# Two-term operands in every fourth value block, values loaded by pairs, the second norm's transposes under the output projection, and finer decode steps, in a hybrid encoder layer with expert retrieval

## Chip, cores and metric

The kernel runs on one core of a Trainium2 chip. The metric is the device time of one execution in microseconds. Its engines are named as in the profile: PE multiplies matrices (PEld loads its weights), DVE and ACT do elementwise work, POOL small elementwise work and the indirect loads, SP issues most transfers. Sixteen transfer engines serve all queues. A change of about 0.2% is the smallest that a measurement of this kernel can tell.

## What is computed

One encoder layer for two sequences of 256 tokens (a prompt, s = 0, and a sample, s = 1), width 1024, all in f32:

```
h = concat(meta, x)                                  # 16 meta tokens ahead, dropped at the end
z = rmsnorm(h) @ w_in                                # conv gates and q, k, v
y = concat(norm(gated_conv3(z)), norm(attention(z))) # 8 heads, 2 kv heads
h = h + y @ w_out
xn = rmsnorm(h)                                      # the second norm
s = einsum(xn @ wq, subkeys)                         # 8 heads x 2 halves x 128 keys
top 16 of each half, top 16 of the 256 sums          # picks 16 of 16384 experts per head
gates = softmax(picked scores)
a = gelu(u[idx] . xn) * gates                        # 128 experts per token
h = h + sum(a * v[idx])
```

u and v are tables of 16384 x 1024 f32, 67 MB each. The scores decide which experts are picked, so they need close to f32 accuracy.

## The kernel before

The two sequences take different ways through the expert tables.

**Sequence 0, gathered.** For each token tile of 128 tokens (t = 0, 1) and each of its 128 picks per token, one indirect load (L157) brings 128 rows of 8 KB (a row of u and of v side by side) into a ring of GBUF = 4 buffers. DVE takes the dot with x (`g_dot`, tile grow), ACT the gelu and the gate (`g_weight`, tile dots), DVE adds the value row times the weight to hg (`g_val`). That makes 256 gathers. They are spread over the whole of the work for sequence 1: `bg(us)` stands behind each piece of PE work, adds us times a share to a credit, and calls `gather()` for each GU = 2.65 of it. The first call fills the ring; each later one does one dot, the value of the gather before it, and one issue. Each issue also waits for the last matmul recorded in `pe_mark`. After the last dot and value of t = 0 the accumulator is stored, and x and hg are loaded anew for t = 1, by POOL (L166 to L168, L190).

**Sequence 1, dense.** All 16384 experts are computed: block j of 128 has 16 PE instructions pSj = u_j x (the u loop, L867), gelu on ACT, a product with the gate matrix A(j); then in the v loop (L893) acc += A(j) v_j, four f32 matmuls of 128x512, which are eight PE instructions of two passes each. The gate matrix is scattered from the picks by `gates_dense` (L802): decode of the picks for both tiles, then 64 steps that build one-hot operands on DVE and multiply them on PE (pgm, L848).

**Order.** The instruction order within each engine is what the code emits, with a planner that may move ready work ahead; a gather's dot is pinned behind DVE's last instruction emitted before it. Long work for DVE is written as generators with a price at each `yield`: `run_tasks` goes on with the task while a second credit is not negative. The stages are: front(0) with operands split in two f32r terms (three products, one pass each, in place of the f32 pair of two passes), projections and top-k of sequence 0; front(1) with gathers at share SF = 0.5 and top-k and decode of tile 1 as a task at SB0 = 0.35; the projections of sequence 1 (share SR = 0.6) with step1 for the top-k of each head; the u loop with share SS = 0.64 (0.7 once the dense steps are done) and the dense steps at SBS = 0.42; the v loop, in which the remaining gathers (`left`) are dealt out evenly over 126 blocks.

**Second norm.** At the end of `front`, four slices of w_out (L676) are added to h; in the last slice `hold` keeps gathers back, the sum of squares gives the scale, DVE forms x = h * scale * g (L696), and `norm_T` (L698) turns it: 16 PE transposes (pt, L416) with ACT copies to xr, and for s = 0 the low term xrl on DVE. Then the projections `pqq` with wq start.

**Buffers.** Weights, u blocks and most v blocks share four buffers of 4 KB per partition (`wtile`); every third v block is in one of two buffers vp, so six in all. The S accumulators of the u loop have four PSUM buffers.

```
875          n = tau[0]
876          if n:
877              act.activation(p[:, :n], p[:, :n], AF.Gelu)
878              dve.tensor_tensor(A(j)[:, :n], p[:, :n], A(j)[:, :n], op=ALU.mult)
904          want = left * (j + 1) // (P - 2)
905          while done < want:
906              gather()
```

Of the kernel before, what the change touches and what calls it, by code (L numbers as in the profile page):

```python
# [18 lines left out]
P = 128  # L19
# [20 lines left out]
SS = 0.64  # L40
SMAX = 0.7
SBS = 0.42


@with_exitstack
def encoder_layer(ctx: ExitStack, tc: tile.TileContext, xp, xs_, meta, vec, w_in, w_out, wq,
# [25 lines left out]
    def sb(name, bufs, side="left"):  # L72
        return tc.tile_pool(name=name, bufs=bufs, side=side, reuse_waits="tile")
# [5 lines left out]
    drm = ctx.enter_context(tc.tile_pool(name="drm", bufs=1, space=DRAM))  # L79
    wp = ctx.enter_context(sb("wp", 4))  # L80
    selp = ctx.enter_context(sb("sel", 1, "right"))
    gc = ctx.enter_context(sb("gc", 1, "right"))
    ga = ctx.enter_context(sb("ga", GBUF, "right"))

    ident = cst.tile([P, P], F32, name="ident")
# [126 lines left out]
    GU = 2.65  # L212
    hold = [False]

# [7 lines left out]
    def bg(us):  # L222
        if tasks:
            credit["b"] += us * share["b"]
            run_tasks(1)
        credit["a"] += us * (share["a"] if tasks else min(share["a"] + share["b"], SMAX))
        while credit["a"] >= GU and not hold[0]:
            credit["a"] -= GU
            gather()


    def retrieval(pools, sv, si, cv, cp, gs, scores, t0, lkbuf, dc):

# [29 lines left out]

        def gates(t):
            ge_ = gate_all[:, t0 + t].rearrange("p (h k) -> p h k", k=KTOP)
            dve.tensor_tensor(ge_, cv[:, t], cv[:, t, :, 0:1].to_broadcast([P, PH, KTOP]), op=ALU.subtract)
            act.activation(gate_all[:, t0 + t], gate_all[:, t0 + t], AF.Exp)
            dve.tensor_reduce(gs[:, t], ge_, axis=AX.X, op=ALU.add)
            dve.reciprocal(gs[:, t], gs[:, t])
            dve.tensor_tensor(ge_, ge_, gs[:, t, :, None].to_broadcast([P, PH, KTOP]), op=ALU.mult)  # L270

        def lookup(mask, tab2, out):
            w = lkbuf(0)
            if tab2 is None:
# [12 lines left out]

        def decode(t):
            s16 = t2.tile([P, 16, KTOP], F16, tag="s16", name="s16", bufs=1)
            dve.tensor_copy(s16, si[:, t])  # L290
            c16 = t2.tile([P, PH, KTOP], F16, tag="c16", name="c16", bufs=1)
            dve.tensor_copy(c16, cp[:, t])
            s4 = s16.rearrange("p (h q) k -> p h q k", q=2)
            di = t2.tile([P, PH, KTOP, 2], F16, tag="di", name="di", bufs=1)
            dj = t2.tile([P, PH, KTOP, 2], F16, tag="dj", name="dj", bufs=1)
            for r in range(2):
                dve.tensor_copy(di[:, :, 0, r], s4[:, :, 0, 0])
                dve.tensor_tensor(di[:, :, 1:, r], s4[:, :, 0, 1:], s4[:, :, 0, :-1], op=ALU.subtract)
# [4 lines left out]
            lookup(mk, di, idx_i[:, t].rearrange("p (h k) -> p h k", k=KTOP))  # L303
            yield 6.0
            b16 = t2.tile([P, PH, KTOP], F16, tag="b16", name="b16", bufs=1)
            lookup(mk, None, b16)
            dve.tensor_tensor(b16, c16, b16, op=ALU.subtract)
            yield 4.0
# [3 lines left out]
            lookup(mk2, dj, idx_j[:, t].rearrange("p (h k) -> p h k", k=KTOP))  # L312
# [23 lines left out]

    def projections(xr, sk, scores, qp, step=None, split=False):

        late = []

        def key_scores(hp, qs):
            pn = pst.tile([P, 2, P], F32, tag="tr", name="pn")
            for t in range(2):
                pe.matmul(pn[:, t, :], qs[:, t * P:(t + 1) * P], sk[:, hp, :], start=True, stop=True)
            act.activation(scores[:, hp], pn, AF.Copy)
            if step is not None and hp % 2:
                step(hp // 2)

        for hd in range(PH):
            w = weights(wq, hd, split)  # L350
            for pp in range(2):
# [69 lines left out]

    def front(s, h):

# [249 lines left out]
        if sp:  # L673
            xrl = [r0t.tile([P, 4, 256], F32R, tag=f"lk{i}", name=f"xrl{i}", bufs=1) for i in range(2)]
        xs2 = []
        for sl in range(4):  # L676
            hold[0] = sl == 3
            w = weights(w_out, sl, sp)
            for t in range(2):
# [5 lines left out]
                act.activation(sq, hsl, AF.Square, accum_out=ss2[:, t, sl:sl + 1])  # L685
                bg(3.5)
                if sl == 3:
                    sst = tmp.tile([P, 2], F32, tag="sst", name="sst")
                    dve.tensor_reduce(sst[:, 0:1], ss2[:, t], axis=AX.X, op=ALU.add)
                    rsqrt(sst[:, 1:2], sst[:, 0:1], 1, 1.0 / D)  # L690
                    if s == 0 and t == 0:
                        x = gc.tile([P, D], F32, tag="xg", name="xg0")
                        gctx["x"] = x
                    else:
                        x = tmp.tile([P, D], F32, tag="xs", name="xs")
                    dve.scalar_tensor_tensor(x, h[:, t, :], sst[:, 1:2], gf, op0=ALU.mult, op1=ALU.mult)  # L696
                    xs2.append(x)
        for t in range(2):  # L698
            tok = slice(t * P, (t + 1) * P)
            norm_T(lambda c: xr[:, c, tok], xs2[t], (lambda c: xrl[c.start // 4][:, :, tok]) if sp else None)  # L700
        hold[0] = False
        if s == 0:
# [11 lines left out]

    xr0 = front(0, hs_)

# [16 lines left out]

    heads0, fin0, _ = retrieval(r0t, *picks(r0p, "p0"), sc0, 0, lk0, dc0)

# [16 lines left out]
    share.update(a=SF, b=SB0)  # L752
    xr1 = front(1, hs1)

# [33 lines left out]
    def step1(hd):  # L788
        for _ in heads1(hd, [0, 1]):
            pass  # L790
        topk_left[0] -= 1

    share.update(a=SR, b=0.0)
    projections(xr1, sk1, sc1, q1, step1)
    pfs.close()
# [94 lines left out]
    hd_ = gc.tile([P, 2, D], F32, tag="xr", name="hd")  # L890
    left = len(queue) + len(pend)
    done = 0
    for j in range(P):  # L893
        vb = vp.tile([P, D], F32, tag="v", name="v") if j % 3 == 2 else wtile("v")
        nc.sync.dma_start(vb, vn3[:, j])
        if j == P // 2:
            for t in range(2):
                act.dma_start(hd_[:, t, :], hdram[1 + t])
        for t in range(2):
            for q in range(2):  # L900
                i = pe.matmul(acc[t][q], A(j)[:, t * P:(t + 1) * P], vb[:, q * 512:(q + 1) * 512],  # L901
                              start=j == 0, stop=j == P - 1, skip_group_check=True)
# [80 lines left out]
```

## Time and profile before

| what | value |
|---|---|
| median of 3 runs | 1390.26 us (1388.64 to 1391.82) |
| profiled execution, its own time | 1388.95 us |
| its span, first to last instruction | 1387.0 us |
| PE busy, share of the span | 1309.7 us, 94% |
| DVE busy | 1032.9 us, 74% |
| ACT, POOL busy | 433.9 us, 424.7 us |
| moved by transfers | 460.19 MB, mean 332 GB/s |
| granted PE clock, mean | 0.984 |

The shares are means over stages with different limits, so the page's totals don't tell what one stage waits for. The stages by time: front(0) and its projections to about 200 us, front(1) to about 340, the projections of sequence 1 to about 414, the u loop to 924, the v loop to 1383. Times in the rows of a timeline are us from the span's start; in brackets stands how long the engine was idle before, and on whose end.

### The profile page before, as it was taken

The page shows a single profiled execution, that of the slowest core. Times are in us where ns is not written, and L with a number is a line of the kernel's source. Part 1 is how long each engine was busy: PE and PEld are TensorE (multiplying, and loading weights), DVE is VectorE, ACT ScalarE, POOL GpSimd, SP SyncE. Part 2 cuts the span into 40 slices and gives each one's busy share as a digit, 9 for nine tenths or more (in the row PEclk, how much of TensorE's full clock was granted, in tenths as well). Part 3 has the DMA queues.
Part 4 walks back from the last instruction along what each step waited for, and adds up shares of the span by engine and source line. Part 5 has one row for each costly group of instructions (what it writes and reads, how often), then busy time and mean ns, then how long its engine had stood idle before and what let it go on. Part 6 is the DMA issues. An engine that isn't in the chain of part 4 may idle for free. (4 is left out here: it accounts for less than half of the span.)

```text
span 1387.0 us, 17651 instructions
## 1 busy us (share of the span) xinstructions
PE 1309.7 (94%) x5868; PEld 931.2 (67%) x5868; DVE 1032.9 (74%) x2349; ACT 433.9 (31%) x1456; POOL 424.7 (31%) x481
## 2 busy tenths in 40 slices
PE   5998998998989997799999999989999999999998
PEld 5888996676868886688888888854443334444433
DVE  5656899785899785888888899476666666666665
ACT  4554532732222211455555544121111111111111
POOL 2111124341344322212222222233454543334431
PEclk9999999999999999899999999999999999999999
DMA  6434536578888998799999999999999999999997
GB/s 213 128 120 136 181 113 237 211 274 313 311 309 296 409 396 305 305 365 358 363 361 359 371 357 388 366 417 417 416 417 416 417 417 416 416 417 415 417 417 311
DMA packets 90234, 460.19 MB, mean 332 GB/s; under 512 B 10512, under 2 KB 11024, under 8 KB 57120
## 3 DMA queue, kind: packets, MB, share of 16 engines
q0 software_dynamic: 37296, 270.02, 49.0%
q1 hardware_dynamic: 50832, 182.33, 35.5%
q10 hardware_dynamic: 2016, 6.72, 1.4%
q8 instruction: 46, 0.75, 0.2%
q14 instruction: 44, 0.36, 0.1%
HBM read 454.81 MB, written 4.19 MB: 331 GB/s over the span
## 5 line engine op out<-in xcount | busy, mean ns | idle before, releaser
L157 POOL DMA_INDIRECT grow<-in_uv,eidx x256 | 345.6, 1350 | 692.6 <-DMA grow<-in_uv,eidx 142.4
L130 PE MATMUL pSj<-xr,u 128*128 128x256 f32 x2048 | 466.2, 385 | 10.6 <-ACT Al L63 6.6
L130 PEld LDWEIGHTS pSj<-xr,u 128*128 128x128 f32 x2048 | 387.7, 192 | 65.2 <-ACT Al L63 8.7
L63 DVE SCALAR_TENSOR_TENSOR grow<-grow,xg 128x1024 f32<-128x1024 f32 x256 | 312.4, 1221 | 149.5 <-DMA grow<-in_uv,eidx 145.6
L63 DVE SCALAR_TENSOR_TENSOR hg<-grow,dots,hg 128x1024 f32<-128x1024 f32 x256 | 328.0, 1281 | 80.0 <-ACT dots L63 77.6
L901 PE MATMUL acc<-v,Al 128*128 128x512 f32 x752 | 335.4, 599 | 3.3
L901 PEld LDWEIGHTS acc<-v,Al 128*128 128x128 f32 x752 | 138.9, 190 | 199.2 <-issue 154.3
L63 ACT ACTIVATE dots<-dots 128x1 f32<-128x1 f32 x256 | 51.5, 202 | 564.8 <-DVE grow L63 564.6
L901 PE MATMUL acc<-v,Ah 128*128 128x512 f32 x272 | 119.1, 596 | 1.4 <-DMA v<-in_v_n 1.0
L901 PEld LDWEIGHTS acc<-v,Ah 128*128 128x128 f32 x272 | 50.8, 190 | 69.8 <-issue 58.8
L63 ACT ACTIVATE gl<-oj,glo 128x128 f16<-128x128 f16 x256 | 89.1, 393 | 12.0 <-DVE oj L63 5.8
L63 ACT ACTIVATE dots<-dots,gate_all 128x1 f32<-128x1 f32 x256 | 75.0, 294 | 7.4 <-ACT dots L63 0.4
L63 ACT ACTIVATE pSj<-pSj 128x256 f32<-128x256 f32 (+40 forms) x93 | 26.1, 281 | 126.2 <-PE pSj L130 126.2
L63 DVE TENSOR_TENSOR wlo<-w,whi 128x1024 fp32r<-128x1024 f32 x42 | 51.0, 1217 | 19.1 <-ACT whi L63 13.1
L130 PE MATMUL pqq<-xr,w 128*128 128x256 f32 x256 | 59.8, 388 | 0.0
L130 PEld LDWEIGHTS pqq<-xr,w 128*128 128x128 f32 x256 | 48.8, 196 | 6.7 <-ACT xr L63 0.2
L63 ACT ACTIVATE whi<-w 128x1024 fp32r<-128x1024 f32 x42 | 44.0, 1056 | 23.2 <-PE pqq L130 12.2
L848 PE MATMUL pgm<-gh,oi 128*128 128x128 f16 x256 | 35.9, 220 | 13.7 <-DVE gh L63 13.6
L130 PE MATMUL pc<-xT,w 128*128 128x258 f32 (+1 forms) x192 | 47.4, 390 | 1.1 <-DVE rb L63 0.6
L130 PEld LDWEIGHTS pc<-xT,w 128*128 128x128 f32 x192 | 34.8, 191 | 8.7 <-issue 2.5
L130 PE MATMUL pqq<-xr,whi 128*128 128x256 f32 x128 | 37.6, 297 | 0.0
L130 PE MATMUL pqq<-xrl,whi 128*128 128x256 f32 x128 | 36.7, 287 | 0.0
(261 smaller groups left out, 1536.1 us busy)
## 6 DMA issues: line engine op xcount, KB each, us to landing
u<-in_u_t SPq DMA_DIRECT2D x128, 512.0 KB
v<-in_v_n SPq DMA_DIRECT2D x128, 512.0 KB
w<-in_w_in SPq DMA_DIRECT2D x36, 512.0 KB
w<-in_wq SPq DMA_DIRECT2D x32, 512.0 KB
w<-in_w_out SPq DMA_DIRECT2D x16, 512.0 KB
grow<-in_uv,eidx POOLq DMA_INDIRECT x256
hdram<-h ACTq DMA_DIRECT2D x3, 512.0 KB
h<-in_xp SPq DMA_DIRECT2D x2, 512.0 KB
```

Source lines behind the costliest of these rows:

```text
L63: i = f(*a, **k)
L130: i = pe.matmul(out, st_(c, a), mv(c, b), start=(n == 0), stop=(n == NC * len(terms) - 1))
L157: i = pool.indirect_dma_start(out=r, out_offset=None, in_=uv, in_offset=bass.IndirectOffsetOnAxis(ap=eidx[:, t, k:k + 1], axis=0))
L848: pe.matmul(pg[:, r, :], oi[:, k, :], gh[:, k, :], start=True, stop=False)
L901: i = pe.matmul(acc[t][q], A(j)[:, t * P:(t + 1) * P], vb[:, q * 512:(q + 1) * 512], start=j == 0, stop=j == P - 1, skip_group_check=True)
```

## The change

1. In the v loop every fourth block (j % 4 == 3) has A(j) and v_j in two f32r terms each, high and low, and three products of one pass each: 12 matmuls in place of eight instructions. ACT makes the high terms, DVE the low ones, one block ahead of PE.
2. Two v blocks are loaded by one transfer (8 KB per partition), into three buffers of that size; the weight buffers are closed before the v loop.
3. At the end of `front` the transposes take h itself, slice by slice, under the next slice's matmuls (`turn`); the gain goes in as a scale of the copy on ACT, and the row scale rn later: for s = 0 in the softmax of the gates, for s = 1 by `rescale`, which scales the first two key scores on copying and then multiplies xr in place by the scale, broadcast over partitions by a matmul. `hold` is gone; x is only formed for s = 0.
4. `decode` yields after smaller pieces.
5. In the projections of sequence 1 the steps of step1 give the gathers' credit (`more`), and `bg` gives none from the first of them on.
6. hd is loaded at the end of the v loop.

```diff
+SPL = 4
...
+    def more(us):
+        credit["a"] += us
+        while credit["a"] >= GU:
             credit["a"] -= GU
             gather()
...
-            act.activation(gate_all[:, t0 + t], gate_all[:, t0 + t], AF.Exp)
+            act.activation(gate_all[:, t0 + t], gate_all[:, t0 + t], AF.Exp, scale=1.0 if rn is None else rn[:, t:t + 1])
...
+            yield 2.4
             n = 8
             while n > 1:
                 dve.tensor_tensor(w[:, :, 0:n, :], w[:, :, 0:n, :], w[:, :, n:2 * n, :], op=ALU.add)
                 n //= 2
             dve.tensor_tensor(out, w[:, :, 0, :], w[:, :, 1, :], op=ALU.add)
+            yield 1.6
...
+            yield 1.8
             mk = lkbuf(1)
...
-            yield 6.0
+            yield from lookup(mk, di, idx_i[:, t].rearrange("p (h k) -> p h k", k=KTOP))
...
-            yield 5.0
+            yield 0.3
...
+            if hp < 2 and rn is not None:
+                for t in range(2):
+                    act.activation(scores[:, hp, t], pn[:, t], AF.Copy, scale=rn[:, t:t + 1])
+            else:
+                act.activation(scores[:, hp], pn, AF.Copy)
...
+                if hd == 0 and rescale is not None:
+                    rn = rescale(xr, pp)
                 bg(3.9)
...
+        def turn(sl):
+
+            pt = pst.tile([P, 2, 256], F32, tag="tr", name="pt")
+            for c in range(2):
+                for t in range(2):
+                    o = (2 * sl + c) * P
+                    pe.transpose(pt[:, c, t * P:(t + 1) * P], h[:, t, o:o + P], ident)
+            for c in range(2):
+                k = 2 * sl + c
+                act.activation(xr[:, k], pt[:, c], AF.Copy, scale=vecs[:, 8 + k:9 + k])
+                if sp:
+                    dve.scalar_tensor_tensor(xrl[k // 4][:, k % 4], pt[:, c], vecs[:, 8 + k:9 + k], xr[:, k].bitcast(F32),
+                                             op0=ALU.mult, op1=ALU.subtract)
+
         for sl in range(4):
-            hold[0] = sl == 3
...
-                bg(3.5)
...
+                if t == 0 and sl:
+                    turn(sl - 1)
+                if sl < 3 or t == 0:
+                    bg(3.5)
+        turn(3)
         for t in range(2):
...
+            dve.tensor_reduce(rn[:, t:t + 1], ss2[:, t], axis=AX.X, op=ALU.add)
+        rsqrt(rn, rn, 2, 1.0 / D)
+        bg(3.5)
...
     def step1(hd):
-        for _ in heads1(hd, [0, 1]):
-            pass
+        share["a"] = 0.0
+        for us in heads1(hd, [0, 1]):
+            more(us * SR)
...
+    def rescale(xr, pp):
+
+        if pp == 0:
+            on = q1.tile([P, P], F32, name="on", bufs=1)
+            pool.memset(on, 1.0)
+            dg = q1.tile([P, 2, P], F32, name="dg", bufs=1)
+            for t in range(2):
+                act.activation(dg[:, t], ident, AF.Copy, scale=rn1[:, t:t + 1])
+            pb = pss.tile([P, 512], F32, tag="sc", name="pb")[:, :256]
+            pe.matmul(pb, on, dg.rearrange("p t n -> p (t n)"), start=True, stop=True)
+            rows.append(pb)
+        else:
+            for c in range(NC):
+                dve.tensor_tensor(xr(c), rows[0], xr(c), op=ALU.mult)
+        return rn1
...
-    vp = ctx.enter_context(sb("vp", 2, "right"))
+    wpx.close()
+    vp = ctx.enter_context(sb("vp", 3, "right"))
+    ap_ = ctx.enter_context(sb("ap", 1, "right"))
...
+    def values(j):
+
+        if j % 2 == 0:
+            vpair[0] = vp.tile([P, 2, D], F32, tag="v", name="v") if j else v0
+            nc.sync.dma_start(vpair[0], vn3[:, j:j + 2])
+        vb = vpair[0][:, j % 2]
+        if j % SPL != SPL - 1:
+            return ((A(j), vb),)
+        vh, vl = vhl[:, 0], vhl[:, 1]
+        ah = ap_.tile([P, 256], F32R, tag="ah", name="ah")
+        al = ap_.tile([P, 256], F32R, tag="al", name="al")
+        act.activation(ah, A(j), AF.Copy)
+        act.activation(vh, vb, AF.Copy)
+        dve.tensor_tensor(al, A(j), ah.bitcast(F32), op=ALU.subtract)
+        dve.tensor_tensor(vl, vb, vh.bitcast(F32), op=ALU.subtract)
+        return ((ah, vh), (al, vh), (ah, vl))
+
+    nxt = values(0)
     for j in range(P):
-        vb = vp.tile([P, D], F32, tag="v", name="v") if j % 3 == 2 else wtile("v")
-        nc.sync.dma_start(vb, vn3[:, j])
...
+        terms = nxt
+        nxt = values(j + 1) if j + 1 < P else None
+        for n, (a, v) in enumerate(terms):
             for t in range(2):
+                for q in range(2):
+                    i = pe.matmul(acc[t][q], a[:, t * P:(t + 1) * P], v[:, q * 512:(q + 1) * 512],
+                                  start=j == 0 and n == 0, stop=j == P - 1 and n == len(terms) - 1, skip_group_check=True)
...
+    hd_ = vp.tile([P, 2, D], F32, tag="v", name="hd")
+    nc.sync.dma_start(hd_, hdram[1:3].rearrange("t p d -> p t d"))
```

More of the change, by code (lines that the diff above doesn't have):

```diff
@@ L79, in encoder_layer @@
     drm = ctx.enter_context(tc.tile_pool(name="drm", bufs=1, space=DRAM))
-    wp = ctx.enter_context(sb("wp", 4))
     selp = ctx.enter_context(sb("sel", 1, "right"))
@@ L83, in encoder_layer @@
     ga = ctx.enter_context(sb("ga", GBUF, "right"))
+    wpx = ExitStack()
+    wp = wpx.enter_context(sb("wp", 4, "right"))
     ident = cst.tile([P, P], F32, name="ident")
@@ L212, in encoder_layer @@
     GU = 2.65
-    hold = [False]
     def run_tasks(limit=None):
@@ L226, in bg, with retrieval @@
         credit["a"] += us * (share["a"] if tasks else min(share["a"] + share["b"], SMAX))
-        while credit["a"] >= GU and not hold[0]:
+        more(0.0)
+    def more(us):
+        credit["a"] += us
+        while credit["a"] >= GU:
             credit["a"] -= GU
             gather()
-    def retrieval(pools, sv, si, cv, cp, gs, scores, t0, lkbuf, dc):
+    def retrieval(pools, sv, si, cv, cp, gs, scores, t0, lkbuf, dc, rn=None):
         t2 = pools
@@ L302, in decode @@
                               dc[:, 0:1].to_broadcast([P, PH, 16, 16]), op=ALU.is_ge)
-            lookup(mk, di, idx_i[:, t].rearrange("p (h k) -> p h k", k=KTOP))
-            yield 6.0
+            yield from lookup(mk, di, idx_i[:, t].rearrange("p (h k) -> p h k", k=KTOP))
             b16 = t2.tile([P, PH, KTOP], F16, tag="b16", name="b16", bufs=1)
-            lookup(mk, None, b16)
+            yield from lookup(mk, None, b16)
             dve.tensor_tensor(b16, c16, b16, op=ALU.subtract)
-            yield 4.0
             mk2 = lkbuf(1)
@@ L311, in decode @@
                               dc[:, 2:3].to_broadcast([P, PH, 16, 16]), op=ALU.is_equal)
-            lookup(mk2, dj, idx_j[:, t].rearrange("p (h k) -> p h k", k=KTOP))
+            yield from lookup(mk2, dj, idx_j[:, t].rearrange("p (h k) -> p h k", k=KTOP))
             if t0 == 0:
                 dve.scalar_tensor_tensor(eidx[:, t], idx_i[:, t], 128.0, idx_j[:, t], op0=ALU.mult, op1=ALU.add)
-            yield 5.0
+            yield 0.3
         def head_steps(hd, tiles):
@@ L335, in retrieval, with projections @@
         return head_steps, fin_steps, all_steps
-    def projections(xr, sk, scores, qp, step=None, split=False):
+    def projections(xr, sk, scores, qp, step=None, split=False, rescale=None):
+        rn = None
         late = []
@@ L344, in key_scores @@
                 pe.matmul(pn[:, t, :], qs[:, t * P:(t + 1) * P], sk[:, hp, :], start=True, stop=True)
-            act.activation(scores[:, hp], pn, AF.Copy)
+            if hp < 2 and rn is not None:
[3 more added lines that the diff above has]
+                act.activation(scores[:, hp], pn, AF.Copy)
             if step is not None and hp % 2:
@@ L420, in norm_T, with front @@
                 dve.tensor_tensor(dst_lo(cs), pt, dst(cs).bitcast(F32), op=ALU.subtract)
-    def front(s, h):
+    def front(s, h, rn):
         sp = s == 0
@@ L674, in front @@
             xrl = [r0t.tile([P, 4, 256], F32R, tag=f"lk{i}", name=f"xrl{i}", bufs=1) for i in range(2)]
-        xs2 = []
+        def turn(sl):
[10 more added lines that the diff above has]
+                                             op0=ALU.mult, op1=ALU.subtract)
         for sl in range(4):
-            hold[0] = sl == 3
             w = weights(w_out, sl, sp)
@@ L685, in front @@
                 act.activation(sq, hsl, AF.Square, accum_out=ss2[:, t, sl:sl + 1])
-                bg(3.5)
[L687 to L697, printed above, removed]
-        for t in range(2):
-            tok = slice(t * P, (t + 1) * P)
-            norm_T(lambda c: xr[:, c, tok], xs2[t], (lambda c: xrl[c.start // 4][:, :, tok]) if sp else None)
-        hold[0] = False
+                if t == 0 and sl:
[3 more added lines that the diff above has]
+        turn(3)
+        for t in range(2):
+            dve.tensor_reduce(rn[:, t:t + 1], ss2[:, t], axis=AX.X, op=ALU.add)
+        rsqrt(rn, rn, 2, 1.0 / D)
+        bg(3.5)
+        xs2 = []
+        if s == 0:
+            for t in range(2):
+                x = gc.tile([P, D], F32, tag="xg", name="xg0") if t == 0 else tmp.tile([P, D], F32, tag="xs", name="xs")
+                dve.scalar_tensor_tensor(x, h[:, t, :], rn[:, t:t + 1], gf, op0=ALU.mult, op1=ALU.mult)
+                xs2.append(x)
+            gctx["x"] = xs2[0]
         if s == 0:
@@ L713, in front @@
         return lambda c, k=0: xr[:, c]
-    xr0 = front(0, hs_)
+    rn0 = r0p.tile([P, 2], F32, name="rn0")
+    xr0 = front(0, hs_, rn0)
     hs1 = one.tile([P, 2, D], F32, tag="h", name="h1")
@@ L732, in lk0 @@
         return r0t.tile([P, PH, 16, 16], F16, tag=f"lk{i}", name=f"lk{i}", bufs=1)
-    heads0, fin0, _ = retrieval(r0t, *picks(r0p, "p0"), sc0, 0, lk0, dc0)
+    heads0, fin0, _ = retrieval(r0t, *picks(r0p, "p0"), sc0, 0, lk0, dc0, rn0)
     def step0(hd):
@@ L752, in encoder_layer @@
     share.update(a=SF, b=SB0)
-    xr1 = front(1, hs1)
+    rn1 = selp.tile([P, 2], F32, name="rn1")
+    xr1 = front(1, hs1, rn1)
     pf.close()
@@ L788, in step1 @@
     def step1(hd):
-        for _ in heads1(hd, [0, 1]):
-            pass
+        share["a"] = 0.0
+        for us in heads1(hd, [0, 1]):
+            more(us * SR)
         topk_left[0] -= 1
+    rows = []
+    def rescale(xr, pp):
[3 more added lines that the diff above has]
+            dg = q1.tile([P, 2, P], F32, name="dg", bufs=1)
+            for t in range(2):
+                act.activation(dg[:, t], ident, AF.Copy, scale=rn1[:, t:t + 1])
[6 more added lines that the diff above has]
+        return rn1
     share.update(a=SR, b=0.0)
-    projections(xr1, sk1, sc1, q1, step1)
+    projections(xr1, sk1, sc1, q1, step1, rescale=rescale)
     pfs.close()
@@ L889, in encoder_layer @@
     vn3 = v_n.rearrange("(i j) d -> i j d", j=P)
-    hd_ = gc.tile([P, 2, D], F32, tag="xr", name="hd")
+    vhl = gc.tile([P, 2, D], F32R, tag="xr", name="vhl")
     left = len(queue) + len(pend)
     done = 0
+    v0 = [vp.tile([P, 2, D], F32, tag="v", name="v") for _ in range(3)][-1]
+    vpair = [v0]
+    def values(j):
[14 more added lines that the diff above has]
+    nxt = values(0)
     for j in range(P):
-        vb = vp.tile([P, D], F32, tag="v", name="v") if j % 3 == 2 else wtile("v")
-        nc.sync.dma_start(vb, vn3[:, j])
-        if j == P // 2:
+        terms = nxt
+        nxt = values(j + 1) if j + 1 < P else None
+        for n, (a, v) in enumerate(terms):
             for t in range(2):
[L898 to L902, printed above, removed]
+                for q in range(2):
+                    i = pe.matmul(acc[t][q], a[:, t * P:(t + 1) * P], v[:, q * 512:(q + 1) * 512],
+                                  start=j == 0 and n == 0, stop=j == P - 1 and n == len(terms) - 1, skip_group_check=True)
         pe_mark[0] = i
```

## The prediction

> **What bounds the kernel now.** I read the busy times by stretches first (stretch, length, busy us with instruction count of PE, PEld, DVE, ACT, POOL, then granted clock, DMA share, GB/s), then the chain that ended last.
>
> ```profile
> 160.00:180.00 20.00, 20.00 (x173) 20.00 (x172) 19.79 (x100) 10.28 (x20) 3.58 (x21) 1.00 0.54 159
> 340.00:440.00 100.00, 92.35 (x437) 80.43 (x438) 89.77 (x435) 23.05 (x76) 38.24 (x73) 0.95 0.82 301
> 600.00:860.00 260.00, 259.93 (x1513) 226.74 (x1512) 228.86 (x466) 135.77 (x562) 58.08 (x58) 1.00 0.96 363
> 923.96:1372.00 448.04, 443.42 (x1001) 185.07 (x999) 291.81 (x350) 57.49 (x232) 187.16 (x115) 1.00 1.02 417
> ```
>
> The u loop (600 to 860) is PE's: no idle, 363 GB/s. The v loop begins at 923.96, and there both are full: PE nearly so, the transfers at a share of 1.02 and 417 GB/s. Which of them sets its end? The chain (start, length, what):
>
> ```profile
> 1046.38 3.71 PE acc L901 x8
> 1050.09 0.02 issue
> 1050.11 18.90 DMA v<-in_v_n
> ...
> 1270.18 58.65 PE acc L901 x136
> ...
> 1383.22 0.69 DVE hd L63
> ```
>
> Unhindered, an instruction takes 58.65/136 = 0.431 us, a block of eight 3.45, 128 blocks 441.6. The loop takes 1383.2 - 924.0 = 459.2, so PE's own floor is 17.6 us below it. What stands between is a landing of v: 18.90 and then 3.71 of one block, 22.7 us for the six buffers, 3.78 us a block. Now the bytes (counts from the loop's tiles):
>
> ```profile
> L157 POOL DMA_INDIRECT grow<-in_uv,eidx x115: 936/1910/1959, 925.1 to 1365.7; - x115
> ...
> L895 SPq DMA_DIRECT2D v<-in_v_n x123: 327/328/328, 924.2 to 1362.1; - x123
> ```
>
> 123 loads of 0.524 MB and 115 gathers of 1.049 MB (128 rows of 8 KB) are 185 MB; 417 GB/s for 448.0 us moves 187 (hd is most of the rest). **The transfers bound the v loop**, and PE comes 4% behind them. Time is gained there by moving bytes ahead of it, hardly by a faster PE.
>
> **The change, part by part**, against the profiled execution's 1388.95 us (its span of 1387.0 and 1.95 around it); the median of the runs, 1390.26, is 1.3 higher.
>
> *Fewer gathers in the v loop.* A gather is called for each 2.65 us of credit. Before: front 1 gives 107.2 x 0.5 = 53.6, the projections 16 x 3.9 x 0.6 = 37.4, the u loop 114 x 2.24 + 14 x 2.45 = 289.7 (0.64 x 3.5 a block while dense steps last, then 0.7 x 3.5). 380.7/2.65 is 143 calls, of which the first only issues: 142 done, 114 left. After: the steps of step1 give 8 x (2.9 + 2.9 + 3.5) x 0.6 = 44.6, and bg only its first two calls, 4.7; decode's yields sum to 14.1 for 15, so the dense steps end at block 112, not 114, and the u loop gives 290.1. 393.0/2.65 is 148 calls, 109 left. **Five gathers, 5.24 MB at 417 GB/s: -12.6 us.** Without hold, two calls only come somewhat earlier.
>
> *Operands in two terms.* 32 blocks get 12 matmuls for 8 instructions. A single pass of 512 columns is not in the trace. The first row above has 20/173 = 0.116 us for 256 columns in one pass; so 0.116 and 0.431 bound it, and I take 0.216, half the f32 instruction (nearest, with the same 512 columns, and about twice 0.116). 12 x 0.216 = 2.59 for 3.45: PE's floor falls by 27.5 to 414 us. While the transfers need about 435 I cost it at nothing. What it adds on other engines, by rows of the same shapes:
>
> ```profile
> L63 DVE TENSOR_TENSOR wlo<-w,whi 128x1024 fp32r<-128x1024 f32 x42 | 51.0, 1217 | 19.1 <-ACT whi L63 13.1 <-PE pc L130 5.6
> ...
> L63 ACT ACTIVATE whi<-w 128x1024 fp32r<-128x1024 f32 x42 | 44.0, 1056 | 23.2 <-PE pqq L130 12.2 <-PE pc L130 3.2 <-PE po L130 3.0
> ...
> L63 DVE TENSOR_TENSOR h<-po,h 128x256 f32<-128x256 f32 x16 | 6.5, 419 | 6.5 <-PE po L130 6.5
> ```
>
> ACT 1.06 and some 0.4 for ah, DVE 1.22 + 0.42 = 1.64. DVE's cycle of a gather:
>
> ```profile
> 1043.56 1.22 DVE L63 SCALAR_TENSOR_TENSOR grow<-grow,xg 128x1024 f32<-128x1024 f32 x1 [0.66 <-DMA grow<-in_uv,eidx]
> 1044.71 0.08 DVE L63 DVE_READ_ACCUMULATOR grow<-grow,xg 128x1 f32 x1
> 1045.39 1.28 DVE L63 SCALAR_TENSOR_TENSOR hg<-grow,dots,hg 128x1024 f32<-128x1024 f32 x1 [0.60 <-ACT dots L63]
> 1047.31 1.22 DVE L63 SCALAR_TENSOR_TENSOR grow<-grow,xg 128x1024 f32<-128x1024 f32 x1 [0.64 <-DMA grow<-in_uv,eidx]
> ```
>
> 3.75 us, of which 3.1 without the wait for the gather. Four blocks hold 3.5 gathers: 10.9, with the split 12.5, of the 4 x 3.4 = 13.6 that the transfers take. It fits, barely. The operands are made one block ahead, and that lead is their cover. The new wait: PE's split block stands behind DVE's queue, where a dot may wait for its gather; PE's next blocks, and the gathers paced by them, stand behind PE. Block 127 is split, so the four accumulators finish together and two of hd's additions of 0.69 lose their cover: +1.4.
>
> *Values by pairs.* As many bytes in half the packets (queue, packets, MB, share of the span's time of 16 engines):
>
> ```profile
> q0 software_dynamic: 37296, 270.02, 49.0%
> q1 hardware_dynamic: 50832, 182.33, 35.5%
> ```
>
> A packet takes 291 ns for 7.24 KB on q0 and 155 for 3.59 on q1; the difference gives 21 ns that don't go with size. 8192 packets fewer x 21/16 = -10.7 at most, nothing at least; as the v loop's 417 GB/s is above what 21 ns would let it have, I take -3. Dots come every 3.75 us and blocks every 3.78: one 4 KB packet of v per 8 KB packet of gather. With equal packets v gets half, PE stops waiting for v, and the gathers end last. PE's 11 us alone after 1372 then shrink to a last dot and its addition: -5 (0 to -8).
>
> The Trainium skill, "DMA: Bandwidth & Descriptors", section "Queues, rings and completion order", says that each engine goes round its queues packet by packet; the two equal periods agree.
>
> *The second norm,* around the end of front 0 and of front 1:
>
> ```profile
> 136.60 1.09 PE L416 MATMUL pt<-ident,xg 128*128 128x128 f32 x8 [1.26 <-DVE xg L63]
> 140.75 1.97 PE L416 MATMUL pt<-ident,xs 128*128 128x128 f32 x8 [3.06 <-DVE xs L63]
> ```
>
> ```profile
> 325.82 9.44 PE L130 MATMUL po<-w,catT 128*128 128x256 f32 x43
> 336.83 1.07 PE L416 MATMUL pt<-ident,xs 128*128 128x128 f32 x8 [1.56 <-DVE xs L63]
> 340.87 1.97 PE L416 MATMUL pt<-ident,xs 128*128 128x128 f32 x8 [2.97 <-DVE xs L63]
> ```
>
> PE waits 4.3 and 4.5 us; the transposes are only moved. One addition (0.42) with its hand-overs stays ahead of the last four transposes, 1.5 to 2 us: -2.5 each. In front 1, rescale takes back 1: a broadcast matmul (2 x 0.22) and the first of eight DVE products on PSUM (0.42), the others running under 16 x 0.22 of PE. A gather, no longer held, may stand ahead of the last addition. **-4** (0 to -9). Dropping x there frees 2 x 1.28 of DVE.
>
> *Projections, small decode steps.* Two more gathers (5 us of DVE) and the products (3.4) go where DVE is busy 89.77 of 100 us. What is late next is the first dense step:
>
> ```profile
> 563.35 0.26 PE L848 MATMUL pgm<-gh,oi 128*128 128x128 f16 x1 [13.63 <-DVE gh L63]
> ```
>
> PE, ahead of DVE, stops 13.6 us. Small steps keep decode from delaying gathers in bursts; the new DVE work, and one u block more behind the stop (dense steps begin after block 33, not 34), take that back. 0, bounds -13.6 (no stop) and +12 (8.4 of DVE and a block of 3.7).
>
> *The switch of token tiles,* on POOL, DVE and PE:
>
> ```profile
> 878.19 1.14 POOL L157 DMA_INDIRECT grow<-in_uv,eidx  x1 [0.30 <-issue]
> 884.41 0.57 POOL L168 DMA_DIRECT2D hg<-hdram  x1 [5.07 <-DMA out_yp<-hg]
> 893.01 1.39 POOL L157 DMA_INDIRECT grow<-in_uv,eidx  x1 [8.04 <-DVE hg L63]
> ```
>
> ```profile
> 887.94 1.23 DVE L63 SCALAR_TENSOR_TENSOR grow<-grow,xg 128x1024 f32<-128x1024 f32 x1 [6.01 <-DMA grow<-in_uv,eidx]
> ...
> 900.45 1.23 DVE L63 SCALAR_TENSOR_TENSOR grow<-grow,xg 128x1024 f32<-128x1024 f32 x1 [3.63 <-DMA grow<-in_uv,eidx]
> ```
>
> ```profile
> 903.95 3.72 PE L130 MATMUL pSj<-xr,u 128*128 128x256 f32 x16 [2.16 <-DVE Ah L63]
> 908.21 3.72 PE L130 MATMUL pSj<-xr,u 128*128 128x256 f32 x16 [0.54 <-DVE Ah L63]
> 913.19 10.93 PE L130 MATMUL pSj<-xr,u 128*128 128x256 f32 x48 [1.26 <-DVE Ah L63]
> ```
>
> POOL issues no gather for 14.8 us; DVE loses 9.6, PE only 4.0, covered by four S buffers. By the credits this falls at block 111 now and at 106 after, where dense steps run on to 110 and PE needs DVE in each: +3 (0 to 9.6 - 4.0 = 5.6).
>
> **Sum:** -12.6 + 1.4 - 3 - 5 - 4 + 0 + 3 = -20.2, so 1368.8; beside the median, 1.3 higher: **1370**.
>
> **Rivals.** *The first dense step's stop goes* (20%): 1370 - 13.6 = 1356. For it: decode's bursts on DVE. Against: DVE waits for gathers there as well, and gets more of them.
>
> *Pairs raise the rate* (8%): all of the 10.7, 1362. Against: 417 GB/s is flat with half-size loads. The same page, section "Bandwidth", asks for loads of 1 MiB and gives a ceiling of 435 GB/s; by it 435 us of transfers would shrink by some 18, an estimate.
>
> *New DVE work is shown* (14%): the u loop starts 12 us later, 1382. For it: DVE at 90% there.
>
> *Split operands come late* (10%), the slower side: if vh, vl and al (1.06 + 1.22 + 0.42 = 2.7) stand bare ahead of each split block, four blocks cost 3 x 3.45 + 2.59 + 2.7 = 15.6, and the kernel 1370 + 32 x (15.6 - 13.6) = 1434. The transfers cover 13.6 - 12.9 = 0.7 of it and the gain of 20 another 0.6: from 1.3 bare it is slower. Against: a block of lead, 3.45.
>
> **Numbers.** Forecast 48%, the rivals 20, 8, 14 and 10. The range, 1346 to 1390, reaches below the first rival to the lower bounds of the tails and up to no gain; it leaves out the last rival and some of the low end. Faster by over 0.2%, about what can be told from no change: 84; within it 6 (4 of the third rival, 2 of the forecast); slower 10.
>
> **What would show it.** Right: the v loop near 440 us at about 417 GB/s, PE's gaps in it at split blocks, behind DVE, none on v; pt under po, PE idle some 2 us before pqq; the stop before the first pgm above 8 us; the switch's gap on PE at 5 to 10 us. Wrong: a v loop still at 459, or PE waiting over 1.3 us at each split block.

## The result and the profile after

The changed kernel takes 1369.01 us (median of 4 runs, 1365.08 to 1374.20), the kernel before 1391.04 (4 runs); ratio 0.9844, 95% interval 0.9803 to 0.9885. Forecast were 1370 us and a range of 1346 to 1390. The profiled execution took 1366.6 us, its span is 1364.8, 22.2 shorter than that of before.

First where the stages begin and end. The groups of the u loop's weight loads (line, engine, operation, count: duration ns min/median/max, first and last start in us, then the form), of before and of after:

```profile
L130 PEld LDWEIGHTS pSj<-xr,u x2048: 186/190/338, 414.8 to 923.5; 128*128 128x128 f32 x187
```

```profile
L132 PEld LDWEIGHTS pSj<-xr,u x2048: 186/190/338, 405.0 to 911.1; 128*128 128x128 f32 x187
```

The u loop starts 9.8 us earlier and is 2.6 shorter (506.1 for 508.7). The v loop then takes 1360.7 - 911.5 = 449.2 to the end of the last addition, for 1383.9 - 924.0 = 459.9 (the 459.2 of the forecast end at that addition's start). So the 22.2 are about 10, 2.5 and 10.5, less 1 behind the last addition. The forecast's steps had them as 4 (front and projections), -3 (the u loop longer, by the switch) and 19.2 (v loop). Each is a difference of two single profiles: over the six profiles of the changed kernel and of experiments with the same code up to there, the u loop starts at 400.2 to 410.3, 405.1 on the mean.

The busy times by stretches of after (stretch, length, busy us with count of PE, PEld, DVE, ACT, POOL, granted clock, DMA share, GB/s):

```profile
340.00:440.00 100.00, 98.03 (x475) 85.59 (x474) 93.50 (x429) 22.17 (x80) 43.33 (x76) 0.98 0.90 338
600.00:860.00 260.00, 257.92 (x1485) 224.61 (x1484) 217.85 (x441) 130.87 (x532) 56.26 (x57) 0.99 0.95 361
911.50:950.00 38.50, 28.32 (x74) 14.62 (x73) 27.12 (x36) 7.22 (x23) 10.72 (x10) 0.91 0.96 384
1000.00:1340.00 340.00, 329.71 (x899) 168.48 (x898) 249.80 (x310) 74.25 (x223) 102.37 (x86) 1.00 1.01 421
911.50:1360.70 449.20, 425.34 (x1153) 216.94 (x1151) 329.52 (x412) 96.56 (x291) 129.93 (x111) 0.99 0.99 412
```

PE fills 98 us of 340 to 440, where it filled 92. In the v loop the transfers are still full, at 421 GB/s for 417; only its first 38.5 us are not (384). The last row counts 111 gathers issued in the loop (POOL), before it was 115. The bytes fit: 64 loads and 111 gathers of 1.049 MB each are 183.5 MB, 436 us at 421 GB/s.

PE's waits of over 0.1 us from 395 to 960 (engine, what waited, on whom, us in total, times, longest), before and after:

```profile
PE pgm L848 <- DVE gh L63: 13.6, 1, 13.6
PE pSj L130 <- ACT Al L63: 6.6, 4, 2.9
PE pn L344 <- ACT qs L63: 5.5, 2, 4.7
PE pSj L130 <- DVE Ah L63: 4.0, 3, 2.2
```

```profile
PE pSj L132 <- ACT Al L64: 9.3, 6, 3.5
PE acc L970 <- ACT vhl L64: 8.2, 1, 8.2
PE pi L866 <- DVE ident L64: 8.0, 1, 8.0
PE pgm L896 <- DVE gh L64: 2.1, 1, 2.1
PE acc L970 <- DVE al L64: 2.0, 1, 2.0
PE pn L352 <- ACT qs L64: 0.6, 1, 0.6
PE pSj L132 <- DVE Ah L64: 0.2, 1, 0.2
```

The stop before the first dense step is still there under two names: 8.0 us for the f16 identity, with which the picks are turned, and 2.1 for the first gh, 10.1 for 13.6. The u loop's waits for ACT (Al), all ahead of that stop, take back 2.7 (9.3 for 6.6). The projections' wait of 4.7 (pn, the key scores) is gone, the switch of token tiles costs PE 0.2 for 4.0. New is a wait of 8.2 us at the first split block, PE's timeline of after (start, length, group, and in brackets the idle time before it):

```profile
911.50 10.46 PE L970 MATMUL acc<-v,Al 128*128 128x512 f32 x24
930.19 2.08 PE L970 MATMUL acc<-vhl,ah 128*128 128x512 f32 x4 [8.22 <-ACT vhl L64]
932.06 1.77 PE L970 MATMUL acc<-vhl,al 128*128 128x512 f32 x4
933.67 1.10 PE L970 MATMUL acc<-vhl,ah 128*128 128x512 f32 x4
...
948.98 1.09 PE L970 MATMUL acc<-vhl,ah 128*128 128x512 f32 x4
949.90 10.46 PE L970 MATMUL acc<-v,Al 128*128 128x512 f32 x24
```

Three whole blocks, then the operands of the fourth are not ready: the products with A of the last u blocks and four gathers still stand in the queues of DVE and ACT. The stop costs more than its 8.2 us: the granted clock behind it is 0.50 from 930 to 932 and 0.62 from 932 to 934, and the first two groups of four matmuls take 1.87 and 1.61 us from start to start, for 0.92 at a clock of 1.00, 1.6 more together. At full clock four one-pass matmuls take 949.90 - 948.98 = 0.92, 0.23 each; I had taken 0.216. A split block is 2.76 us for 3.44 (439.75/128, from a run below), and PE's floor 96 x 3.44 + 32 x 2.76 = 418. Later in the loop PE's waits are short; PE's waits of after, from 895 to the end, have

```profile
PE acc L970 <- DVE al L64: 13.4, 14, 2.0
```

The queues (packets, MB, share of 16 engines), and how the chain that ended last closes (start, length, what), both of after:

```profile
q0 software_dynamic: 37296, 270.02, 49.7%
q1 hardware_dynamic: 41888, 183.37, 35.7%
```

```profile
1344.11 11.04 DMA grow<-in_uv,eidx
1356.80 1.44 PE acc L970 x5
1358.26 1.29 DVE hd L64 x2
```

q1 carries about the same bytes in 50832 - 41888 = 8944 packets fewer. The chain now ends with a landing gather, not with a landing v: its dot, behind it on DVE the last block's al, eight matmuls, hd. PE's timeline has the wait for that al:

```profile
1356.80 1.19 PE L970 MATMUL acc<-vhl,al 128*128 128x512 f32 x4 [0.78 <-DVE al L64]
```

### The profile page after: what moved, and what is told of

It reads as the page before. It is cut to its first block, busy times and chain, and to the rows that moved or that the text cites. A ratio compares the mean times of both kernels' runs of the same rounds, so it can differ in the third digit from the quotient of the medians.

```text
span 1364.8 us, 17980 instructions
## 1 busy us (share of the span) xinstructions
PE 1284.2 (94%) x5998; PEld 959.9 (70%) x5998; DVE 1072.0 (79%) x2420; ACT 478.3 (35%) x1531; POOL 372.9 (27%) x480
## 3 DMA queue, kind: packets, MB, share of 16 engines
q1 hardware_dynamic: 41888, 183.37, 35.7%
## 5 line engine op out<-in xcount | busy, mean ns | idle before, releaser
L159 POOL DMA_INDIRECT grow<-in_uv,eidx x256 | 290.7, 1136 | 737.8 <-DVE hg L64 144.4
L132 PEld LDWEIGHTS pSj<-xr,u 128*128 128x128 f32 x2048 | 388.1, 193 | 66.1 <-ACT Al L64 13.6
L970 PE MATMUL acc<-v,Al 128*128 128x512 f32 x568 | 247.6, 592 | 0.0
L970 PEld LDWEIGHTS acc<-v,Al 128*128 128x128 f32 x568 | 107.8, 190 | 126.4 <-issue 124.4
L970 PE MATMUL acc<-vhl,ah 128*128 128x512 f32 x256 | 82.5, 444 | 8.6 <-ACT vhl L64 8.2
L970 PE MATMUL acc<-v,Ah 128*128 128x512 f32 x200 | 87.3, 592 | 0.0
L970 PEld LDWEIGHTS acc<-vhl,ah 128*128 128x128 f32 x256 | 48.5, 190 | 32.9 <-issue 12.7
L970 PEld LDWEIGHTS acc<-v,Ah 128*128 128x128 f32 x200 | 38.0, 190 | 44.7 <-issue 44.0
L64 ACT ACTIVATE pSj<-pSj 128x256 f32<-128x256 f32 (+39 forms) x94 | 26.6, 284 | 106.9 <-PE pSj L132 106.9
L970 PE MATMUL acc<-vhl,al 128*128 128x512 f32 x128 | 37.6, 416 | 13.5 <-DVE al L64 13.4
```

The costliest lines, as they stand in the source:

```text
L64: i = f(*a, **k)
L132: i = pe.matmul(out, st_(c, a), mv(c, b), start=(n == 0), stop=(n == NC * len(terms) - 1))
L159: i = pool.indirect_dma_start(out=r, out_offset=None, in_=uv, in_offset=bass.IndirectOffsetOnAxis(ap=eidx[:, t, k:k + 1], axis=0))
L970: i = pe.matmul(acc[t][q], a[:, t * P:(t + 1) * P], v[:, q * 512:(q + 1) * 512], start=j == 0 and n == 0, stop=j == P - 1 and n == len(ter ...
```

## The experiments

Each undoes or adds one thing in the changed kernel, and is compared with the kernel before on the same chip. Differences between experiments are differences of these ratios times 1389 us. They ran in three groups on three chips; across groups the kernel before is the common measure. The changed kernel itself was run again with the first group only (no split, single blocks, the credit):

> The changed kernel once more, as the measure for the other kernels on the same chip. Both theories: 1369 us, 0.984 of the kernel before.

It took 1363.79 us, ratio 0.9820 (0.9803 to 0.9836): the reference for all that follows. In its profile the u loop is at 410.3 to 915.8 and the stops are those of above (8.2 for the identity, 2.2 for gh, 7.7 at the first split block). The stages ahead of the u loop vary by 5 us to either side between profiles of the same code, so small effects there are read from the medians.

**No block in two terms.**

```diff
-        if j % SPL != SPL - 1:
+        if True:
             return ((A(j), vb),)
```

> The changed kernel without operands in two terms: all 128 value blocks as f32 pairs. Theory A (transfers bound the value loop): within 4 us of the changed kernel, with the loop's rate still near 420 GB/s and no PE gap at every fourth block. Theory B (PE bounds the value loop, the split pays for itself): 27.5 us slower, 32 blocks x 0.86 us, about 1396 us.

1363.20 us, 0.9815 (0.9792 to 0.9839): the split is worth nothing here, as forecast, but not only for the reason given. The stretch of the v loop without split, PE's last group in its timeline, and the end of the chain:

```profile
942.00:1320.00 378.00, 378.00 (x882) 167.39 (x881) 241.96 (x289) 47.74 (x192) 119.24 (x96) 1.00 1.01 421
```

```profile
1317.60 25.05 PE L970 MATMUL acc<-v,Ah 128*128 128x512 f32 x58
```

```profile
1345.71 1.00 issue
1346.71 0.09 DVE grow L64
```

PE has no idle time at all, is through at 1342.65 (439.7 us after 903.0, its floor for f32), and the remaining gathers keep DVE busy to 1351. With the split PE has slack and waits; both ways end 448 to 449 us after the start of the loop. Two bounds lie within a few us of each other, the transfers' 436 and PE's 440.

**Values by single blocks.** Each block of the pair is loaded by its own transfer into its half of the same buffer.

```diff
-            nc.sync.dma_start(vpair[0], vn3[:, j:j + 2])
+            pass
         vb = vpair[0][:, j % 2]
+        nc.sync.dma_start(vb, vn3[:, j])
```

> The changed kernel with each value block loaded by a transfer of its own, 4 KB per partition, into the same buffers. Theory A with equal packets not mattering: 0 to +3 us, the loop's rate back from 421 to 417 GB/s (438 us x 1% = 4 us). Rival (21 ns per packet that do not go with size): +10.7 us. In both PE waits for values again, since v gets one 4 KB packet per 8 KB packet of gather.

1370.52 us, 0.9851 (0.9829 to 0.9873): +4.3 us, with intervals that overlap a little. The rate in the middle of the loop falls; from 950 to 1340, first with pairs (the changed kernel run again), then without:

```profile
950.00:1340.00 390.00, 375.72 (x1024) 191.88 (x1023) 286.11 (x356) 84.35 (x254) 114.58 (x99) 1.00 1.01 421
```

```profile
950.00:1340.00 390.00, 376.57 (x1017) 193.76 (x1016) 281.86 (x349) 84.02 (x250) 129.38 (x98) 0.99 1.01 414
```

At 421 for 417, the rate of before with loads of this size, 183.5 MB take 4.2 us less; the 414 holds one slow stretch (1100 to 1150 at 399 GB/s, all others 416 or 417). The pairs are worth about 4 by the rate, and the times, with intervals that overlap, don't contradict it. Against what both theories said, PE itself waits for no v here either. But the loads land a median of 12.7 us after their issue, for 9.8 with pairs, and landings of v are back in the chain: ACT's copies vhl wait for them, 26 times, where in the changed kernel they never do.

**The gathers' credit in the projections as before.**

```diff
-        share["a"] = 0.0
-        for us in heads1(hd, [0, 1]):
-            more(us * SR)
+        for _ in heads1(hd, [0, 1]):
+            pass
```

> The changed kernel with the gathers of the projections paid as before: 16 calls of 3.9 us x 0.6 in place of the steps of the top-k. 114 gathers left for the value loop in place of 109. Theory A: +12.6 us (5 x 1.049 MB at 417 GB/s), about 1382 us, the value loop longer by that and the projections unchanged or up to 5 us longer. Theory B: 0 in the value loop, whatever changes is in the projections.

1392.41 us, 1.0016 (0.9994 to 1.0037): +27 us, twice what five gathers weigh. All that the change gains is gone with this one edit. PE's waits of this kernel, from 395 to 960, then from 895 on:

```profile
PE pgm L895 <- DVE gh L64: 17.2, 1, 17.2
PE pSj L132 <- DVE Ah L64: 6.6, 4, 3.4
PE pSj L132 <- ACT Al L64: 5.6, 4, 3.9
PE pn L352 <- ACT qs L64: 4.7, 1, 4.7
```

```profile
PE acc L969 <- DVE al L64: 22.4, 16, 4.6
```

The first dense step's stop is 17.2 for 10.1, the switch 6.6 for 0.2, the projections wait 4.7 again, and in the v loop PE waits longer for low terms. The v loop is 15 us longer, the u loop 8 (407.2 to 921.1). A theory, not shown by this run: DVE is late everywhere by the gathers that it did not do in the projections. Two runs ask which of this is whose.

**That credit, and no split.** Both edits of above together.

> The changed kernel with the credit of the projections as before (114 gathers left for the v loop) and no block in two terms. Giving the credit back alone cost 27 us, where its bytes explain 12.6, and PE waited there some 24 us for low terms in 17 places. Theory A: part of the 27 is the split blocks, which wait for DVE when more gathers fill the loop; without them the kernel is 5 to 12 us faster, 1380 to 1387. Theory B: those waits only mirror the transfers, as without the credit's edit, where leaving the split out made no difference: 1390 to 1394.

1385.68 us, 0.9965 (0.9945 to 0.9986): 7 us faster than with the split. Theory A holds: with five gathers more in the loop the split costs time. From 1200 to 1300, with split and without:

```profile
1200.00:1300.00 100.00, 92.40 (x247) 47.53 (x246) 72.58 (x92) 21.81 (x66) 31.95 (x25) 0.97 0.99 401
```

```profile
1200.00:1300.00 100.00, 100.00 (x234) 44.27 (x233) 63.25 (x78) 12.93 (x52) 28.88 (x25) 1.00 1.01 421
```

A PE that waits for DVE delays the gathers' issues, which wait for PE's marks: in these 100 us POOL waits 32.9 us for PE's matmuls with the split and 11.0 without. It is the stretch where the rates differ most; from 950 to 1350 it is 414 GB/s for 421, some 7 us. This is the rival "split operands come late" in small.

The pair also divides the 27. Without the split, undoing the credit costs 0.9965 - 0.9815, 21 us: the v loop is 460.2 us for 448.1, 12.1 longer, what five gathers weigh. The split adds 7. The rest, some 8 or 9, arises ahead of the v loop: the u loop's last group starts at 921.1 and 916.0 in the two profiles with the old credit, and at 902.6 to 915.8, 909.6 on the mean, in the four with the new credit and the same shares (the changed kernel twice, no split, single blocks).

**That credit, and the old yields of decode.**

> The changed kernel with the credit of the projections as before and with the coarse yields of decode as before. Alone the one cost 27 us and the other 7. If they are separate costs, 1363.8 + 27 + 7 = 1398. If both work through the same stop (DVE late at the first dense step), the second adds nothing: 1390 to 1394.

1388.30 us, 0.9978 (0.9956 to 1.0000): not slower than with the credit's edit alone (1.0016), rather 5 us faster, with intervals that touch. Now the old yields alone:

```diff
-            yield 2.4
             n = 8
...
-            yield 1.6
...
-            yield from lookup(mk, di, idx_i[:, t].rearrange("p (h k) -> p h k", k=KTOP))
+            lookup(mk, di, idx_i[:, t].rearrange("p (h k) -> p h k", k=KTOP))
+            yield 6.0
...
```

> The changed kernel with the decode steps of before (6.0, 4.0 and 5.0). The forecast counted the finer steps at nothing: within 3 us of the changed kernel, the stop ahead of the first dense step as long as it is now (8 to 17 us in all). Rival: the finer steps are what took the 13.6 us stop down, so 5 to 10 us slower.

1371.43 us, 0.9871 (0.9842 to 0.9900): +7 us, where 0 was forecast. Its waits from 395 to 960 begin:

```profile
PE pgm L895 <- DVE gh L64: 13.2, 2, 9.6
PE pSj L132 <- ACT Al L64: 13.1, 6, 4.5
PE pi L865 <- DVE ident L64: 4.7, 1, 4.7
```

13.2 + 4.7 = 17.9 at the first dense step for 10.1. So the two edits aren't separate costs: the stop is 13.6 before, 17.2 without the new credit, 17.9 without the new yields, 15.3 without both, and 10.1 only with both.

**The second norm as before** (x formed first, then the transposes, with `hold`; no `rescale`).

```diff
...
-        turn(3)
...
+            tok = slice(t * P, (t + 1) * P)
+            norm_T(lambda c: xr[:, c, tok], xs2[t], (lambda c: xrl[c.start // 4][:, :, tok]) if sp else None)
...
```

> The changed kernel with the second norm of before: x formed after the whole output projection, then all transposes, gathers held back in the last slice, no rescale. The forecast counted the new form at -4 us (0 to -9): +4 us here, 2.5 at the end of front 0 and 1.5 at the end of front 1. Rival: the 10 us by which the score loop starts earlier in the changed kernel are mostly the norm's: +8 us or more.

1371.30 us, 0.9880 (0.9862 to 0.9898): +8 us, twice the forecast's 4. The first projections start at 143.0 and 346.6 there, at 136.6 and 333.4 in the profile of after. In front 1 PE's timeline of after shows what the planner made of it:

```profile
333.27 0.27 PE L696 MATMUL pt<-ident,h 128*128 128x128 f32 x1
333.38 1.46 PE L132 MATMUL pqq<-xr,w 128*128 128x256 f32 x6
338.47 0.55 PE L696 MATMUL pt<-ident,h 128*128 128x128 f32 x3 [3.63 <-DVE h L64]
```

It put the first six matmuls of pqq, which need only slices turned long ago, ahead of the last three transposes; those then wait 3.63 us, for the last addition behind a gather on DVE. How the 8 divide between the two fronts the profiles can't tell, their early stages vary too much.

**The f16 identity made at the start.** A test of the 8.0 us stop.

```diff
     make_identity(nc, ident)
+    ident16 = cst.tile([P, P], F16, name="ident16")
+    dve.tensor_copy(ident16, ident)
...
-        ident16 = og.tile([P, P], F16, name="ident16")
-        dve.tensor_copy(ident16, ident)
```

> The changed kernel with the f16 copy of the identity made at the start of the kernel; nothing else. PE's wait of 8.0 us for that copy ahead of the first dense step goes. Theory A: PE is the bound of the u loop and it comes 5 to 8 us sooner to the v loop, 1356 to 1359. Theory B: the copy is only the last name in DVE's queue; the first one-hot operands stand behind the same gathers, PE waits for them (pgm behind gh) in its place, within 2 us of 1363.8.

1366.84 us, 0.9823 (0.9790 to 0.9856): no change, theory B. The wait only took another name, in the profile of this kernel:

```profile
PE pgm L896 <- DVE gh L64: 11.4, 2, 9.5
```

11.4 for 8.0 + 2.1. What PE waits for is DVE's queue, the end of decode with gathers between its pieces; the copy was merely the first thing in it with a reader on PE.

**More gathers ahead of the v loop** (SS 0.64 to 0.68, 103 left by the credits), with the split and without:

> The changed kernel with the share of the score loop at 0.68 in place of 0.64: 103 gathers left for the value loop in place of 109. Theory A (transfers bound the value loop): 6 x 1.049 MB at 421 GB/s = -15 us there, down to PE's floor of 414 us and its gaps; the score loop, which moves 363 GB/s, takes them at a cost of 0 to 6 us: 1354 to 1360 us. Theory B (PE bounds it): no gain, 1369 us or more.

> The same share of 0.68, and all value blocks as f32 pairs. Theory A: with the bytes moved away PE's floor of 441.6 us is now the bound, so the loop cannot fall below about 443 us and the kernel is some 10 us slower than with the split at the same share: about 1366 us. Theory B: 27.5 us slower than with the split.

1356.60 us, 0.9777 (0.9756 to 0.9799), and 1362.47 us, 0.9805 (0.9784 to 0.9826). With the split six gathers fewer give -6; without it next to nothing, and the chain says why:

```profile
920.84 439.75 PE acc L970 x1024
```

1024 matmuls in one piece: PE is the bound there, and the transfers fall to 410 GB/s in 930 to 1330. The split is worth 4 (by the ratios) to 6 us (by the medians) once the bytes no longer bind, though the intervals just overlap.

**One step further**: SS 0.70, SMAX 0.74 (99 left), the identity early, the first split block at j = 11.

> The changed kernel with SS 0.70 and SMAX 0.74 (99 gathers left by the credits, where 109 were), the f16 identity made at the start, and the first split block at j = 11 instead of 3. With SS 0.68 alone 1356.6 was measured, so 103 gathers. If PE can still follow at a floor of 414 + 1.7, four gathers fewer give -10 and the first block's wait of 8.2 goes: 1340 to 1350. If DVE in the u loop is full (PE there waits longer for the gated products), the loop grows by what the v loop loses: 1354 to 1360.

1364.36 us, 0.9793 (0.9752 to 0.9834): above both ranges expected, and not better than SS 0.68. The u loop took the gain back, though three edits at once don't tell which of them; its groups and PE's longest waits in it:

```profile
L134 PEld LDWEIGHTS pSj<-xr,u x2048: 186/190/337, 410.0 to 934.6; 128*128 128x128 f32 x187
```

```profile
PE pgm L896 <- DVE gh L64: 26.0, 4, 13.7
PE pSj L134 <- ACT Al L64: 12.6, 7, 4.5
```

The u loop is 524.6 us for 506.1, with 26.0 us of stops behind DVE. From the start of the u loop to the end of the span it is 1364.8 - 405.0 = 959.8 for the change, 949.5 with SS 0.68 (405.6 to 1355.1), 954.5 here. The wait at the first split block is gone as meant (1.4 us is the longest in the v loop). The kernel with SS 0.68 has the lowest ratio of all that ran; its own stop ahead of the first dense step is longer than that of the change, 13.9 + 2.8 = 16.7 us.

## Why the prediction was right, step by step

The sign came out by the mechanism, fewer bytes in a loop that the transfers bound. That the time came within 1 us is luck: the v loop came out 8.5 us longer than forecast, the stages ahead of it 11 us shorter, and the two misses nearly cancel.

| step of the sum | forecast | what the runs showed |
|---|---|---|
| fewer gathers in the v loop | -12.6 | 4 fewer issued in it: 4 x 1.049 MB at 421 GB/s, -10.0; undone alone +27 |
| last block split | +1.4 | not run alone; PE waits 0.8 us there for al, behind the last dot |
| values by pairs | -3 | -4.3 |
| gathers end last | -5 | about -2, the row on the last block included |
| second norm | -4 | -8 (undone alone) |
| projections, small decode steps | 0 | old yields alone +7; the key scores' waits for ACT 6.8 to 0.6 |
| switch of token tiles | +3 | -3.8 |
| operands in two terms | 0 | 0 (its removal 0.0005 faster, within the interval); -4 to -6 with fewer bytes |

**The bound was right.** The v loop stayed with the transfers. Giving PE its f32 work back moved nothing (no split: 0.9815 beside 0.9820), taking bytes away did. What the forecast left out: with 109 gathers left, the transfers' 436 us come to PE's f32 floor of 440, so the bound was about to change hands. The kernels with SS 0.68 show it.

**The v loop came out 8.5 us too long**, 449.2 for 459.9 - 19.2 = 440.7. Of the forecast's own terms the gathers gave 2.6 less, and the end gave 2.2 where -5 and +1.4 make 3.6, so 1.4 less: from the last gather's landing to the last addition it is 1360.7 - 1355.2 = 5.5, since the last split block's al stands behind the last dot. In the kernel before it was 1383.9 - 1376.2 = 7.7, from its last dot in DVE's timeline:

```profile
1376.15 1.23 DVE L63 SCALAR_TENSOR_TENSOR grow<-grow,xg 128x1024 f32<-128x1024 f32 x1 [0.62 <-DMA grow<-in_uv,eidx]
```

The pairs gave 1.3 more. Most of the remainder has a place that the forecast didn't look at, the start: DVE and ACT come to the loop with the last u blocks' products and four gathers undone, PE waits 8.2 us at the first split block, and at 384 GB/s for 38.5 us the transfers lose 38.5 x 37/421 = 3.4. Some 2 us are left whose place is not shown. The forecast had "a block of lead, 3.45" as cover for every split block; for the first it wasn't enough.

**The stages ahead came out 11 us better**, and here the step that failed is "0, bounds -13.6 and +12" for projections and decode, with the credit that the sum priced by bytes alone. Of the 11, 4 are the norm's, which gave 8 for 4. Gathers done between top-k's pieces use DVE while PE works on projections, and PE's stops behind DVE are shorter at the next places where it needs DVE: the first dense step (10.1 for 13.6), the switch (0.2 for 4.0), the split blocks. So undoing the credit costs 27 and not 12.6: 12 for the bytes, 7 for the split blocks, 8 or 9 ahead of the v loop. That a shorter backlog on DVE is what shortens the stops fits these places, but no run isolates it; with SS 0.68, more gathers in the u loop, the first stop is 16.7 us and the kernel still faster. The rival "new DVE work is shown", with a u loop starting 12 us later, is refuted: it starts 9.8 us earlier. The rival "the first dense step's stop goes" came true for 3.5 of its 13.6, of which the waits ahead of it take back 2.7.

**The switch** was put among the last dense steps (block 106 against 110). In the trace the last pgm starts at 851.5, and hg is loaded anew only at 853.5: POOL's timeline of after.

```profile
843.78 0.57 POOL L168 DMA_DIRECT2D out_yp<-hg  x1 [1.90 <-DVE hg L64]
...
853.47 0.57 POOL L170 DMA_DIRECT2D hg<-hdram  x1 [7.83 <-DMA out_yp<-hg]
860.70 1.80 POOL L159 DMA_INDIRECT grow<-in_uv,eidx  x1 [6.67 <-DVE Ah L64]
```

POOL issues no gather for 16 us (14.8 before), but by then PE needs DVE only for the products with A, and four S buffers cover those.

**Split operands come late** was the rival on the slower side, and decided from 1.3 us bare per split block. PE's waits for its operands are 22 us in the loop (8.2 + 13.4 + 0.4), 0.7 a block: below it, and, but for the first block's, covered by the transfers. With five gathers more in the loop they are not covered (7 us, the run without credit and split). The mechanism was right; its distance is five gathers.

**Pairs.** Of 0 to 10.7 I took 3, and 4.3 were measured. The Trainium skill, "DMA: Bandwidth & Descriptors", section "Bandwidth", asks for loads of 1 MiB and gives a ceiling of 435 GB/s; this case's trace had 417 with half a MB and 421 with one, so neither the loss nor the ceiling shows. That v would get half by equal packets fits the traces: PE's waits on v are gone from the chain and the loads land 9.8 us after issue, while with single loads it is 12.7 and v is in the chain again, now by way of ACT. That the packets' size does it, and not the number of loads, is not shown.

**Of the signs named,** these came: gaps of PE at split blocks behind DVE and none on v, pt under po, a stop above 8 us before the first pgm. A wait of 3.6 us came at pqq for the forecast 2, after its first six matmuls instead of ahead of them. The v loop at 440 us and a gap of 5 to 10 us at the switch did not come.

**The parts don't add up.** Undone one at a time they cost 27 + 7 + 8 + 4 = 46 us, together the change gives 25. Undoing the yields costs 7 with the new credit and nothing without it; so at least the first dense step's stop is counted twice.

## What to carry to other kernels

Price an edit that moves work on a shared engine by its queue too, not by the bytes alone: find the next places where the critical engine reads from that queue, and ask how late they are before and after. When two bounds lie within a few per cent, taking work off one shows nothing until the other has moved; test the two edits together before one is judged useless. A wait's name is the first reader in a late queue, and making that one operand early only moves the name.

## What the hardware showed that was not expected

A stop of PE costs more than its length: behind the 8.2 us stop PE ran at a granted clock of 0.50 and then 0.62 for some 3 us and lost 1.6 us more, and in the kernel before, the clock was 0.50 from 555 to 565 and 0.65 from 565 to 570, while PE took up work at 563.35 after its stop of 13.6. A PE that waits long enough lowers the transfers' rate: 401 GB/s for 421 in the 100 us where most was lost, with POOL's issues waiting for PE's marks; in the changed kernel PE's shorter waits left the 421 as it was. An f32r matmul of 512 columns, one instruction, takes 0.23 us, each of the two instructions of an f32 matmul 0.429 (439.75/1024): the three-term block saves a fifth of 3.44 us, not the quarter that I had from half the time. And v's packets of twice the size raised the rate of the loop by only 1%, 417 to 421 GB/s.
